# The fixed order of a state-space layer, rewritten: whole input products between scan and outputs, no row sums in the loop

## The chip, the cores and the metric

The kernel runs on one core of a Trainium2 chip. The metric is device time of one launch in microseconds (us). The core's engines are TensorE (PE, with its weight loads PEld), VectorE (DVE), ScalarE (ACT), GpSimd (POOL) and SyncE (SP), which issues nearly all DMAs of this kernel.

## The reference, cut

A trunk of two layers on x of 512 positions by 1024 columns, float32. Layer 0 mixes with a state-space layer (S5), layer 1 with forgetting attention; each is followed by a gated feed-forward layer with a short convolution. Scales, shifts and gates of every sublayer are a product of the conditioning vector c (adaLN).

```python
def adaln_params(c, w, b):
    mod = jax.nn.silu(c) @ w + b
    shift, scale, gate = jnp.split(mod, 3, axis=-1)

def s5_mixer(h, w_in, lam_re, lam_im, log_dt, b_re, b_im, c_re, c_im, d_skip, w_glu, w_out):
    u = h @ w_in
    ug = u.reshape(Bsz, S, S5_GROUPS, S5_GROUP)      # 64 groups of 16 channels
    ...                                              # lb = exp(lam dt), bb = k(lam, dt) * b, complex
    bu_re = jnp.einsum('blgc,gpc->blgp', u_c, bb_re) # a state of 64 complex numbers per group
    ...                                              # h[t] = lb * h[t-1] + bu[t]
    y = jnp.einsum('blgp,gcp->blgc', hs_re, cr) - jnp.einsum('blgp,gcp->blgc', hs_im, ci)
    y = y + d_skip * u
    y = jax.nn.gelu(y)
    y = y * jax.nn.sigmoid(y @ w_glu)
    return y @ w_out

for i in range(2):
    shift, scale, gate = adaln_params(c, ada_w[i, 0], ada_b[i, 0])
    h = h + gate * mixer_i(modulate(h, norm_g[i, 0], shift, scale))
    shift, scale, gate = adaln_params(c, ada_w[i, 1], ada_b[i, 1])
    h = h + gate * conv_ffn(modulate(h, norm_g[i, 1], shift, scale))
return rmsnorm(h, final_g)
```

## The kernel before

**Products.** Every float32 operand is split into a high part (`w_hi`, `a_xhi`: a rounding copy, mostly on ACT) and a rest (`w_lo`, `x_lo`: source minus high part, on DVE or POOL). A product is three matmuls per tile of 128 x 512: high by high, high by rest, rest by high. With 8 tiles of the inner dimension a 128-column output tile is 24 matmuls; in the state-space layer they are written by `mms` (L323).

**The state-space layer** is `s5`. It is written under a manual schedule: each engine runs its instructions in the order in which the program writes them, SP's DMAs too. SP is one queue: a DMA that waits for something holds up all that is written behind it.

The 1024 columns are 8 tiles m of 8 groups. The scan runs over blocks of 8 positions: 64 blocks a sequence. For each tile there are

- `inputs(m)`: 24 matmuls (L323) make tile m of u; ACT copies it to `uf`, `store_u` sends it to DRAM (`s_ud`), and `turn_u` reads it back turned (`u`). This load waits for the store.
- `s5_made` (L976 on DVE, L980 on POOL): the complex outer products `x` of decay powers and bb; `s5_states_out` (the same lines) those of c, `w2`. `s5_tables` (L966 to L968, POOL) makes the rotation tables in pieces.
- `s5_columns` (L1008, L1011, L1022 on PE): within-block responses and the transposed weights `w1`. ACT copies the first to `ktt`, PE turns it (L1026) to `kt`, SP stores it to DRAM (`s_z`).
- `s5_shifted`: SP loads the shifted response `tw` (L1037) from `s_z`, ACT masks it in 8 pieces to `t` (L1041).
- `s5_scan`: 32 small matmuls (L1053), then nine DVE instructions (L1070 to L1081), among them the scan (L1075), leave the block states `ua`.
- `s5_outputs`: u times t (L1091), w2 times `ua` (L1100), gelu on ACT (`yg`), a store to DRAM (`s_yd`). The gate product reads it back as `yt` (`s5_read_y`) and splits it to `a_hi`/`a_lo`.

The loop over m has one round for each tile. A round also parts one later tile of w_in (`parted`: high part on ACT, L1136, rest on POOL, L1138), and computes adaLN parameters of layer 1: one third as PE steps (`ada_pe`, four matmuls of 32 x 512 for each of the steps, L228), one third as row sums on DVE (`row` loads 512 KB, `row_sum` multiplies and adds, L265). In rounds 6 and 7, and behind the loop, the gate product of the first five output tiles is begun (`glu_head`, L1312), with its weights parted by `gate_hi` (ACT) and `gate_lo` (POOL, L1303). The stage after `s5` ("s5b") finishes the gate product and multiplies by w_out; then come the feed-forward layer, attention and the second feed-forward layer.

Of the kernel before, what the change touches and what calls it, by code (L numbers as in the profile page):

```python
# [63 lines left out]
class Trunk:  # L64
# [6 lines left out]
    def __init__(self, tc, io, ctx):  # L71
# [12 lines left out]
        self.acc = None  # L84
# [103 lines left out]
    def raw(self, shape, src, n=0):  # L188
        if n == 2:
            t = self.rest(shape, F32, "raw")  # L190
        else:
            t = self.wpool.tile(shape, F32, name="raw", tag=("raw", "w_hi")[n], bufs=(RAW, WB)[n])
        self.nc.sync.dma_start(t, src)
        return t
# [92 lines left out]
    def split(self, src, shape, pool=None, bufs=WB, off=None):  # L287
# [9 lines left out]
        self.put_parts(hi, lo, self.raw(shape, src), src if self.by_dma else None)  # L297
# [519 lines left out]
class S5(Trunk):  # L817
# [36 lines left out]
    def s5_params(self, pool, tp, prm, stats):  # L854
# [7 lines left out]
        ring = lambda n: tp.tile([P, (24, 36, 24)[n], H], F32, name=f"s5_ring{n}")  # L862
# [247 lines left out]
    def s5_read_y(self, pool, m, bufs=2):  # L1110
        nc = self.nc
        t = pool.tile([P, L, B], F32, name="yt", bufs=bufs)
        nc.sync.dma_start(t, self.yd[m].rearrange("g c i b -> (g c) i b"))
        return t.rearrange("p i b -> p (i b)")

    def s5(self, i, nxt):
# [5 lines left out]
        with ExitStack() as stack:  # L1122
# [11 lines left out]
            def parted(m):  # L1134
                hi = self.wpool.tile([P, KT, P], F32R, name="w_hi", bufs=WB)
                nc.scalar.activation(hi, w[m], AF.Copy)  # L1136
                lo = self.rest([P, KT, P])
                nc.gpsimd.tensor_tensor(lo, w[m], hi.bitcast(F32), ALU.subtract)  # L1138
                w[m] = [(hi[:, k], lo[:, k]) for k in range(KT)]

            with ExitStack() as start:
# [36 lines left out]
                self.s5_tables(slice(0, 8), 3, 5)  # L1178

                shift = self.ada_pe(i, (0,), late=True)  # L1180
                ps = self.mm.tile([P, S], F32, name="mmp")
                for k in range(KT):
                    if k % 2 == 0:
                        next(shift)
# [9 lines left out]
                load_w(1)  # L1194
# [17 lines left out]
                def part_x(k):  # L1212
                    b = self.par[i][:, k:k + 1]
                    nc.scalar.activation(xhi[:, k], x[:, k], AF.Identity, bias=b)
                    nc.vector.scalar_tensor_tensor(
                        xlo[k], x[:, k], b, xhi[:, k].bitcast(F32), op0=ALU.add, op1=ALU.subtract
                    )

                w2s[0] = self.s5_states_out(0)
                for k in range(3):  # L1220
                    part_x(k)
# [7 lines left out]
                parted(1)  # L1229
                self.s5_tables(slice(0, 8), 5, 6)  # L1230
                ws[0] = next(cols[0])
                for k in range(3, KT):
                    part_x(k)
                self.spread_c()
                self.s5_signs(far)
            pool = self.s5r = spool("s5r", stack)

            def store_u(m, uf):
                nc.sync.dma_start(ud[m].rearrange("g c j b -> (g c) j b"), uf)

            def turn_u(m):
                us[m] = pool.tile([P, GM, B], F32, name="u", bufs=3)
                nc.sync.dma_start(us[m], ud[m].rearrange("g c j b -> (c j) g b"))

            def inputs(m):
                ps = self.mm.tile([P, S], F32, name="mmp")
                for k in range(KT):
                    self.mms(ps, w[m], split_x, k, KT, full)
                    if k == 4:
                        yield  # L1250
# [3 lines left out]
                yield  # L1254

            def shifted_in(m):
                ts[m] = self.s5_shifted(m)
                next(ts[m])

            def scan_in(m):  # L1260
                sts[m] = self.s5_scan(m, ws.pop(m), us[m])
                next(sts[m])

            def made(m):
                xs[m] = self.s5_made(m)

            def columns_in(m):
                cols[m] = self.s5_columns(m, xs.pop(m))
                if m + 1 < KT and m > 1:
                    self.s5_diagonal(m + 1)  # L1270
# [18 lines left out]
            def parts(m, e):  # L1289
                y = yt.pop(m)  # L1290
                nc.scalar.activation(yhi[:, m], y, AF.Copy)
                e.tensor_tensor(ylo[:, m], y, yhi[:, m].bitcast(F32), ALU.subtract)

            def gate_load(n):
                raw[n] = self.raw([P, KT, P], self.io["s5_w_glu"][n], 2 * (n == HEAD - 1))

            def gate_hi(n):
                hi[n] = self.wpool.tile([P, KT, P], F32R, name="w_hi", bufs=WB)
                nc.scalar.activation(hi[n], raw[n], AF.Copy)

            def gate_lo(n):
                lo[n] = self.rest([P, KT, P])
                nc.gpsimd.tensor_tensor(lo[n], raw[n], hi[n].bitcast(F32), ALU.subtract)  # L1303
# [12 lines left out]
            store_u(0, uf)  # L1316
            load_w(2)
            turn_u(0)
            next(cols[0])
            made(1)  # L1320
            shifted_in(0)
            u1 = inputs(1)
            next(u1)
            next(u1)
            load_w(3)
            self.load_c()
            columns_in(1)
            next(ada)
            row()
            turn_u(1)  # L1330
            parted(2)
            scan_in(0)
            ts[0] = next(ts[0])
            for m in range(KT):
                more = m + 1 < KT
                if more:
                    ws[m + 1] = next(cols[m + 1])
                if m + 3 < KT:
                    parted(m + 3)
                if m + 2 < KT:  # L1340
                    up = inputs(m + 2)
                    next(up)
# [4 lines left out]
                if more:  # L1347
# [432 lines left out]
```

## Time and profile before

| | us |
|---|---|
| median of three runs | 1202.3 |
| the three runs | 1200.47, 1202.3, 1207.83 |
| the profiled execution's own time | 1208.57 |
| its span in the trace | 1206.8 |
| PE busy in the span | 1168.7 (97%) |
| DVE, ACT, POOL busy | 956.8, 649.1, 223.9 |
| mean granted clock of PE | 0.982 of full |
| DRAM traffic | 202.72 MB, 168 GB/s |

Durations in the prediction come from the one profiled execution, which is 6.3 us above the median of the runs. In rows of the trace, "L12" is line 12 of the kernel before; names read output <- inputs.

### The profile page before, as it was taken

To read this page: it belongs to the slowest core of one execution; us is meant where nothing else is said; L and a number is where in the kernel's file an instruction comes from. 1 tells how busy PE (TensorE), PEld (TensorE's weight loads), DVE (VectorE), ACT (ScalarE), POOL (GpSimd) and SP (SyncE) were. 2 spreads that over 40 slices of the span, in tenths; PEclk is the share of its full clock that TensorE was granted. 3 is DMA by queue.
4 is the path that set the end of the run, shared out by engine and by line. 5 is a ranking of instruction groups with operands and counts; after the bars stand their busy time and mean duration, and the time that the engine had idled before them with its cause. 6 is when DMAs were issued, how large, how long until landed. Compare 5 with 4: busy or idle time off the path is not lost.

```text
span 1206.8 us, 21348 instructions
## 1 busy us (share of the span) xinstructions
PE 1168.7 (97%) x8223; PEld 1038.5 (86%) x8223; DVE 956.8 (79%) x1733; ACT 649.1 (54%) x1165; POOL 223.9 (19%) x273
## 2 busy tenths in 40 slices
PE   7899987999999999999999999999999999999997
PEld 2577866899999999999899788878999899999987
DVE  8876755979998798887676788876899888898855
ACT  3562452535576666666543566654456555555543
POOL 5677653000011111111000343330000000000000
PEclk9997888999999999999999999999999999999999
DMA  9576576953598898998604654623122332333331
GB/s 353 193 244 206 179 231 217 312 187 102 139 249 239 218 259 230 261 241 230 190 23 132 219 180 162 201 89 93 50 88 93 110 125 86 110 123 92 105 88 71
DMA packets 79717, 202.72 MB, mean 168 GB/s; under 512 B 23951, under 2 KB 26479, under 8 KB 78591
## 3 DMA queue, kind: packets, MB, share of 16 engines
q1 hardware_dynamic: 73135, 181.96, 45.5%
q0 software_dynamic: 6192, 18.88, 9.1%
q8 instruction: 64, 1.05, 0.4%
q10 hardware_dynamic: 288, 0.52, 0.1%
q14 instruction: 38, 0.31, 0.1%
HBM read 194.41 MB, written 6.92 MB: 167 GB/s over the span
## 4 chain that ended last, share of the span: by engine, by line
PE 78%; DVE 11%; DMA 4%; issue 2%; ACT 2%; POOL 2%; SPq 0%; DVEq 0%; POOLq 0%; ACTq 0%
PE mmp L323 39%; PE mmp L583 16%; PE aux L583 6%; PE mmp L1521 3%; DMA raw<-in_w_up 2%; DVE w_lo L307 2%; PE aux L1667 2%; PE aux L1650 1%; PE mmp L1312 1%; DVE sums L554 1%; PE aux L1100 1%; DVE conv L637 1%; PE aux L1620 1%; PE mmp L1156 1%; PE aux L1091 1%
## 5 line engine op out<-in xcount | busy, mean ns | idle before, releaser
L302 ACT ACTIVATE w_hi<-raw 128x1024 fp32r<-128x1024 f32 (+4 forms) x196 | 172.2, 887 | 134.7 <-PE mmp L323 63.9
L307 DVE TENSOR_TENSOR w_lo<-raw,w_hi 128x1024 fp32r<-128x1024 f32 (+4 forms) x153 | 155.1, 1016 | 37.5 <-ACT w_hi L302 33.7
L323 PE MATMUL mmp<-ghi,w_hi 128*128 128x512 f32 (+1 forms) x392 | 144.1, 368 | 0.0
L323 PE MATMUL mmp<-glo,w_hi 128*128 128x512 f32 (+1 forms) x392 | 143.7, 367 | 0.0
L323 PE MATMUL mmp<-ghi,w_lo 128*128 128x512 f32 (+1 forms) x392 | 143.6, 366 | 0.0
L323 PE MATMUL mmp<-a_hi,w_hi 128*128 128x256 f32 (+1 forms) x440 | 141.1, 323 | 0.7 <-ACT nm_t L1435 0.7
L323 PE MATMUL mmp<-a_hi,w_lo 128*128 128x256 f32 (+1 forms) x440 | 139.0, 317 | 0.0
L323 PE MATMUL mmp<-a_lo,w_hi 128*128 128x256 f32 (+1 forms) x440 | 138.8, 316 | 0.0
L583 PE MATMUL mmp<-w_hi 128*128 128x256 f32 x420 | 116.9, 278 | 3.1 <-ACT nm_h L590 3.0
L583 PE MATMUL mmp<-w_hi,w_lo 128*128 128x256 f32 x420 | 116.1, 276 | 0.0
L583 PE MATMUL mmp<-w_lo,w_hi 128*128 128x256 f32 x420 | 116.0, 276 | 0.0
L265 DVE CUSTOM_DVE_ANT_0 ada_raw<-ada_raw,ada_c,rest 128x1024 f32<-128x1024 f32 x72 | 102.1, 1431 | 9.8 <-DMA ada_raw<-in_ada_rows 9.8
L302 ACT ACTIVATE w_hi<-sums 128x1024 fp32r<-128x1024 f32 x78 | 81.8, 1058 | 45.2 <-DVE sums L554 27.8
L307 DVE TENSOR_TENSOR w_lo<-sums,w_hi 128x1024 fp32r<-128x1024 f32 x78 | 94.4, 1219 | 4.5 <-ACT w_hi L302 3.1
L323 PEld LDWEIGHTS mmp<-a_hi,w_hi 128*128 128x128 f32 x440 | 82.2, 188 | 8.2 <-issue 2.6
L323 PEld LDWEIGHTS mmp<-a_hi,w_lo 128*128 128x128 f32 x440 | 82.6, 188 | 6.4
L323 PEld LDWEIGHTS mmp<-a_lo,w_hi 128*128 128x128 f32 x440 | 82.7, 188 | 4.6
L323 PEld LDWEIGHTS mmp<-ghi,w_lo 128*128 128x128 f32 x392 | 73.6, 188 | 12.3
L323 PEld LDWEIGHTS mmp<-ghi,w_hi 128*128 128x128 f32 x392 | 73.6, 188 | 11.2
L323 PEld LDWEIGHTS mmp<-glo,w_hi 128*128 128x128 f32 x392 | 73.6, 188 | 11.1
L583 PEld LDWEIGHTS mmp<-w_hi 128*128 128x128 f32 x420 | 78.8, 188 | 4.5 <-ACT nm_h L590 4.3
L583 PEld LDWEIGHTS mmp<-w_hi,w_lo 128*128 128x128 f32 x420 | 78.8, 188 | 0.1
(332 smaller groups left out, 3196.2 us busy)
## 6 DMA issues: line engine op xcount, KB each, us to landing
raw<-in_w_up SPq DMA_DIRECT2D x88, 512.0 KB, 3.6
ada_raw<-in_ada_rows SPq DMA_DIRECT2D x72, 512.0 KB, 4.8
raw<-in_ada_w SPq DMA_DIRECT2D x24, 512.0 KB, 7.9
raw<-in_w_down SPq DMA_DIRECT2D x32, 384.0 KB, 3.8
raw<-in_w_down SPq DMA_DIRECT2D x32, 320.0 KB, 3.3
nf<-nfd SPq DMA_DIRECT2D x8, 1152.0 KB, 5.7
w_lo<-in_w_up POOLq DMA_DIRECT2D x17, 512.0 KB, 8.2
raw<-in_fox_qk SPq DMA_DIRECT2D x16, 512.0 KB, 3.3
```

The costliest lines, as they stand in the source:

```text
L265: nc.vector.tensor_tensor_reduce(w, w, self.crow, 1.0, self.ada_b[:, i, m:m + 1], ALU.mult, ALU.add, self.par[i][:, m:m + 1])
L302: nc.scalar.activation(hi, src, AF.Copy)
L307: self.late = (nc.vector.tensor_tensor(lo, src, hi.bitcast(F32), ALU.subtract).ins,)
L323: self.last_mm = self.nc.tensor.matmul(o, wt, xt[:, cols], start=(k == 0 and n == 0), stop=(k == nk - 1 and n == 2),)
L554: sub = lambda o, u, v, op=ALU.subtract: nc.vector.tensor_tensor(o, u, v, op)
L583: self.last_mm = nc.tensor.matmul(o, wt[:, k], xt[:, k], start=(first and k == 0 and n == 0), stop=(k == H - 1 and n == 2), skip_group_che ...
L637: nc.vector.scalar_tensor_tensor(t[:, d:], ps[:, :S - d], cw[:, 2 - d, f:f + 1], t[:, d:], op0=ALU.mult, op1=ALU.add)
L1091: nc.tensor.matmul(yp[g2][:, k, :], t[:, 2 * k + g2], u[:, g, :], start=(k == 0), stop=False, skip_group_check=True,)
L1100: nc.tensor.matmul(yp[g2][:, k, 1:], w2[rows, k, r].rearrange("p c i -> p (c i)"), st[rows, r, k, :B - 1], start=False, stop=(r == 1), til ...
L1156: nc.tensor.matmul(ps, self.ones, sq, start=(k == 0), stop=(k == KT - 1))
L1521: self.last_mm = nc.tensor.matmul(ps[q, b][:, :n], xt[:, k, tb], wt, start=(k == 0 and i == 0), stop=(k == KT - 1 and i == 2),)
L1667: nc.tensor.matmul(pv[:, c * P:], self.v[:, hp, k, r].rearrange("p t d -> p (t d)"), pp[:, r, c + 3 * k:NB + 3 * k, :].rearrange("p b t -> ...
```

## The change

It is all in `s5`, but for a few lines that hand things to it:

1. `inputs(m)` is written whole. Before, 15 of its 24 matmuls stood ahead of L1091, and 9 behind L1100.
2. Scale and shift of layer 1 (two thirds) are both computed by PE steps: eight `ada_step`, two in each of the rounds 0 to 2, one in rounds 3 and 4, each with two loads of 512 KB issued two steps ahead. The eight row sums of layer 1 (L265) and their loads are gone; five of layer 0 stay, behind the loop.
3. `rested`, the subtraction on POOL, is written a round behind `parted`, the copy on ACT.
4. The prologue loads and parts w_in tile 1 earlier, sends u of tile 0 earlier, writes inputs(1) ahead of the loop, and has DVE make two of eight `a_xhi`; table pieces of the first tiles move ahead.
5. Loads of gate weights and y for the gate product are written at the start of round 5 (before: rounds 4 and 5, behind other DMAs); their parts are spread over rounds 5 and 6; the rests of y are DVE's, not POOL's. Gate weights 5 to 7 are loaded ahead (`loaded`).

**PE, one round.** In the kernel before, behind the first 15 input matmuls of a round (L323, the names are operands of the split product; L228 is the layer-1 step):

```order
L1026 MATMUL aux<-rest,ktt 128x128
L1091 MATMUL aux<-u,t 128x64 x8
L228 MATMUL mmp<-raw,sc_85 32x512 x4
L1100 MATMUL aux<-ua,w_526 128x63 x16
L323 MATMUL mmp<-a_xhi,w_hi 128x512
L323 MATMUL mmp<-x_lo,w_hi 128x512
L323 MATMUL mmp<-a_xhi,w_lo 128x512
```

In the changed kernel, from the last input matmul of round 1 to the first of round 2 (L1161 is now the step):

```order
L323 MATMUL mmp<-a_xhi,w_lo 128x512
L1026 MATMUL aux<-rest,ktt 128x128
L1091 MATMUL aux<-u,t 128x64 x8
L1100 MATMUL aux<-ua,w_848 128x63 x16
L1161 MATMUL mmp<-raw,sc_85 32x512 x4
L1053 MATMUL aux<-u,w_916 64x64 x16
L1008 MATMUL aux<-dd,rest 128x128
L1011 MATMUL aux<-x,s_cd_133 32x128 x8
L1022 MATMUL aux<-rest,x 128x128 x8
L1161 MATMUL mmp<-raw,sc_85 32x512 x4
L323 MATMUL mmp<-a_xhi,w_hi 128x512
```

The nine matmuls that separated L1100 from the next L1053 now stand ahead of L1026.

**SP, one round.** The DMAs of round 1 before (`in_ada_rows` feeds a row sum, `in_ada_w` a step, `s_w_in` a later inputs):

```order
L193 DMA raw<-in_s_w_in 128x1024
L193 DMA raw<-in_ada_w 128x1024 x2
L258 DMA ada_raw<-in_ada_rows 128x1024
L1107 DMA s_yd<-yg 128x8x64
L1239 DMA s_ud<-uf 128x512
L1000 DMA dd<-in_s_dd 128x128
L1243 DMA u<-s_ud 128x8x64
L1028 DMA s_z<-kt 128x128
L1037 DMA tw<-s_z 128x1024
```

And after (L1260 is the store of u, L1264 its turned load):

```order
L1107 DMA s_yd<-yg 128x8x64
L193 DMA raw<-in_ada_w 128x1024 x2
L1000 DMA dd<-in_s_dd 128x128
L193 DMA raw<-in_ada_w 128x1024 x2
L193 DMA raw<-in_s_w_in 128x1024
L1260 DMA s_ud<-uf 128x512
L1264 DMA u<-s_ud 128x8x64
L1028 DMA s_z<-kt 128x128
L1037 DMA tw<-s_z 128x1024
```

The row sum's load is gone, a second pair of step loads has come, and all loads now stand ahead of the store of u.

**DVE, between two scans.** Before:

```order
L1081 TENSOR_TENSOR ua<-aux,ub 128x512
L976 TENSOR_TENSOR x<-mmp,s_bb 128x1024
L976 TENSOR_TENSOR x_814<-mmp,s_bb 128x1024
L976 TENSOR_TENSOR w_834<-mmp,s_cc 128x1024
L976 TENSOR_TENSOR x_835<-mmp,s_cc 128x1024
L265 ISA ada_raw,par_97<-ada_raw,ada_c,rest 128x1024
L265 ISA par_97 128x1
L1070 TENSOR_TENSOR m_936<-aux,s_rot 128x512
```

After:

```order
L1081 TENSOR_TENSOR ua<-aux,ub 128x512
L976 TENSOR_TENSOR x<-mmp,s_bb 128x1024
L976 TENSOR_TENSOR x_844<-mmp,s_bb 128x1024
L976 TENSOR_TENSOR w_848<-mmp,s_cc 128x1024
L976 TENSOR_TENSOR x_849<-mmp,s_cc 128x1024
L1070 TENSOR_TENSOR m_890<-aux,s_rot 128x512
```

The row sum that stood ahead of the scan's first instruction is gone. Behind `s5` the order of all engines is the same but for the preloaded gate weights.

The diff, cut to its core:

```diff
+            def rested(m):
+                src, hi = w[m]
                 lo = self.rest([P, KT, P])
-                nc.gpsimd.tensor_tensor(lo, w[m], hi.bitcast(F32), ALU.subtract)
+                nc.gpsimd.tensor_tensor(lo, src, hi.bitcast(F32), ALU.subtract)
...
+            def ada_step():
+                k = KT - len(steps)
+                steps.pop()
...
+                for t, wt in enumerate(ada.pop(k)):
+                    for q in range(2):
+                        qq = 2 * t + q
+                        nc.tensor.matmul(
+                            ada["ps"][32 * qq:32 * qq + 32, :], self.sc32[:, k, :], wt[:, q * S:(q + 1) * S],
...
+                if k + 2 < KT:
+                    ada_load(k + 2)
...
-                    if k == 4:
-                        yield
...
-            ada = self.ada_pe(i + 1, (0,), ahead=True)
-            units = [(i + 1, 8 + m) for m in range(8)] + [(i, 16 + m) for m in range(5)]
+            units = [(i, 16 + m) for m in range(5)]
...
             for m in range(KT):
-                more = m + 1 < KT
-                if more:
-                    ws[m + 1] = next(cols[m + 1])
-                if m + 3 < KT:
-                    parted(m + 3)
-                if m + 2 < KT:
-                    up = inputs(m + 2)
-                    next(up)
+                sts[m] = self.s5_scan(m, ws.pop(m), us[m])
+                next(sts[m])
+                ts[m] = next(ts[m])
...
+                if m + 3 < KT:
+                    if m == 0:
+                        parted(3)
+                    rested(m + 3)
...
+                if m == KT - 3:
+                    read(0, 1, 2, 3)
+                    for n in range(3):
+                        gate_load(n)
...
+                sts[m] = next(sts[m])
+                if m == 0:
+                    ada_step()
+                elif m + 1 < KT:
+                    columns_in(m + 1)
+                    if m < 3:
+                        ada_step()
+                if m + 4 < KT:
+                    load_w(m + 4)
+                if m == KT - 3:
+                    gate_hi(0, 1)
+                    gate_lo(nc.gpsimd, 0)
+                if m + 2 < KT:
+                    inputs(m + 2)
+                    turn_u(m + 2)
...
                 outs[m] = self.s5_outputs(m, us.pop(m), ts.pop(m))
                 next(outs[m])
...
-                sts[m] = next(sts[m])
-                if m + 4 < KT:
-                    load_w(m + 4)
-                next(ada, None)
-                next(ada, None)
-                row()
                 outs[m].send((w2s.pop(m), sts.pop(m)))
-                if m + 2 < KT:
-                    made(m + 2)
-                    next(up)
-                    columns_in(m + 2)
...
-                if more:
-                    w2s[m + 1] = self.s5_states_out(m + 1)
-                    row_sum()
-                    scan_in(m + 1)
-                    ts[m + 1] = next(ts[m + 1])
+                if m + 4 < KT:
+                    parted(m + 4)
+                if steps:
+                    ada_step()
+                if m + 2 < KT:
+                    xs[m + 2] = self.s5_made(m + 2)
...
+                if m + 1 < KT:
+                    w2s[m + 1] = self.s5_states_out(m + 1)
+                if m == KT - 3:
+                    y_lo(nc.vector, 0, 1, 2, 3)
+                    gate_lo(nc.gpsimd, 2)
```

More of the change, by code (lines that the diff above doesn't have):

```diff
@@ L296, in split @@
             lo = self.rest(shape, odd=self.odd)
[L297 removed]
+        self.put_parts(hi, lo, self.loaded.pop(0) if self.loaded else self.raw(shape, src), src if self.by_dma else None)
         return hi, lo
@@ L1183, in s5 @@
                     if k % 2 == 0:
+                        next(shift)
+                        if k == KT - 2:
+                            load_w(1)
+                            parted(1)
                         next(shift)
@@ L1287, in read, with y_hi, y_lo, gate_hi @@
                     yt[m] = self.s5_read_y(pool, m, 4)
[L1289 to L1292, printed above, removed]
-            def gate_load(n):
[L1295 to L1303, printed above, removed]
+            def y_hi(*ms):
+                for m in ms:
+                    nc.scalar.activation(yhi[:, m], yt[m], AF.Copy)
+            def y_lo(e, *ms):
+                for m in ms:
+                    e.tensor_tensor(ylo[:, m], yt.pop(m), yhi[:, m].bitcast(F32), ALU.subtract)
+            def gate_load(n):
+                raw[n] = self.raw([P, KT, P], self.io["s5_w_glu"][n])
+            def gate_hi(*ns):
+                for n in ns:
+                    hi[n] = self.wpool.tile([P, KT, P], F32R, name="w_hi", bufs=WB)
+                    nc.scalar.activation(hi[n], raw[n], AF.Copy)
+            def gate_lo(e, *ns):
+                for n in ns:
+                    lo[n] = self.rest([P, KT, P])
+                    e.tensor_tensor(lo[n], raw[n], hi[n].bitcast(F32), ALU.subtract)
             def glu_head(k, part, ms=range(HEAD)):
@@ new lines, in s5 @@
+                    for k in range(4, 6):
+                        glu_head(k, 0)
+                if m + 1 < KT:
+                    if m == 0:
+                        columns_in(1)
+                    next(cols[m + 1])
+                    ts[m + 1] = self.s5_shifted(m + 1)
+                    next(ts[m + 1])
+                if m == KT - 3:
+                    self.rooms, self.rests = WB, 3
+                    yhi = self.normed("a_hi", WHOLE)
+                    ylo = self.normed("a_lo", WHOLE)
+                    y_hi(0, 1, 2, 3)
+                    gate_hi(2)
@@ L1411, in s5 @@
                 glu_head(k, 1)
-            for _ in range(3):
-                row_sum()
-                row()
-            parts(KT - 1, nc.vector)
+            row_sum()
+            row()
+            y_hi(KT - 1)
+            y_lo(nc.vector, KT - 1)
             while rows:
@@ L1418, in s5 @@
                 row()
+            for n in range(HEAD + 1, KT):
+                gate_load(n)
+                self.loaded.append(raw[n])
             gps[HEAD] = self.aux.tile([P, S], F32, name="aux")
@@ L1440, in glu @@
                 )
-            for m in range(HEAD + 1):
-                glu(m, gps[m], slice(0, S))
-            self.product(self.io["s5_w_glu"], range(HEAD + 1, KT), KT, (yhi, ylo), glu, ticks=1)
-            self.load_x(resid)
+            with self.behind(headed):
+                for m in range(HEAD + 1):
+                    glu(m, gps[m], slice(0, S))
+                self.product(self.io["s5_w_glu"], range(HEAD + 1, KT), KT, (yhi, ylo), glu, ticks=1)
+            with self.behind(last_y):
+                self.load_x(resid)
             self.done()
```

188 lines of the change are left out of this document (99 added, 89 removed).

## The prediction

> **What bounds the kernel now.** I read the span first, then one row for each stretch of the program, then the chain that ended last inside the bad stretches, then the waits, then single instructions for prices.
>
> ```profile
> span 1206.8 us, 21348 instructions
> ```
> ```profile
> 38.00:52.20 14.20, 10.97 (x70) 7.69 (x69) 11.56 (x10) 13.13 (x24) 8.97 (x5) 1.00 0.26 79
> 52.20:69.20 17.00, 15.53 (x141) 12.30 (x141) 9.80 (x14) 8.63 (x21) 10.73 (x10) 0.90 0.78 257
> 69.20:83.10 13.90, 13.65 (x140) 10.88 (x139) 13.32 (x17) 7.21 (x20) 12.42 (x7) 1.00 0.69 218
> 83.10:102.30 19.20, 18.29 (x142) 13.79 (x141) 13.81 (x17) 7.18 (x20) 15.11 (x11) 0.75 0.69 222
> 102.30:120.20 17.90, 17.05 (x152) 13.42 (x151) 12.30 (x15) 7.97 (x22) 11.25 (x6) 0.89 0.72 226
> 120.20:136.10 15.90, 15.47 (x133) 12.65 (x133) 12.15 (x15) 7.18 (x20) 9.21 (x9) 0.82 0.54 162
> 136.10:149.90 13.80, 13.80 (x158) 11.92 (x159) 11.42 (x15) 6.86 (x21) 9.15 (x6) 0.96 0.63 194
> 149.90:167.70 17.80, 13.72 (x107) 10.43 (x103) 10.03 (x13) 10.70 (x24) 12.23 (x7) 0.81 0.79 260
> 167.70:206.40 38.70, 32.59 (x186) 25.70 (x184) 19.73 (x24) 10.38 (x24) 17.40 (x13) 0.91 0.64 217
> 206.40:1206.80 1000.40, 987.44 (x6892) 907.83 (x6892) 809.93 (x1452) 558.44 (x949) 95.45 (x131) 1.00 0.52 154
> ```
>
> Columns: from:to, length, busy time of PE, its weight loads, DVE, ACT and POOL (instructions in brackets), granted clock, DMA share, GB/s. Row 1 is the end of the prologue; rows 2 to 7 are rounds 0 to 5 of the state-space loop, cut where L1053 starts; row 8 is round 6, row 9 round 7 with the head of the gate product. The last row is everything else: PE busy 98.7% at full clock, and there the change moves no work, so I put it at zero. What can change lies in the 168 us above it, and shows two losses: PE idles, and its clock falls below 1.00.
>
> The chain of waits names what ends the idle time:
>
> ```profile
> 82.68 2.19 DVE ada_raw L265
> ...
> 150.28 4.71 DMA yt<-s_yd
> ...
> 180.68 8.98 POOL w_lo L1303 x3
> ```
> ```profile
> PE mmp L1312 <- POOL w_lo L1303: 5.8, 3, 2.8
> PE aux L1091 <- DVE ua L1081: 4.1, 4, 2.3
> ```
>
> In the loop a row sum (L265) holds up DVE's scan, and PE stands at L1091/L1100 for its result; in the tail PE stands for the y parts and the gate weights' rests. The four L1091 waits cost 4.1 us as idle time and more as clock:
>
> ```profile
> 90.75 1.97 PE L1091 MATMUL aux<-u,t 128*128 128x64 f32 x16 [0.92 <-DVE ua L1081]
> ```
> ```profile
> 55.00:59.00 4.00, 3.76 (x28) 3.17 (x29) 3.76 (x7) 0.77 (x3) 2.50 (x2) 0.57 1.01 357
> 62.00:69.00 7.00, 7.00 (x66) 5.36 (x64) 2.44 (x3) 2.93 (x5) 5.86 (x8) 1.00 0.63 189
> 92.70:102.90 10.20, 10.20 (x62) 7.09 (x63) 5.45 (x5) 1.14 (x3) 8.81 (x9) 0.50 0.46 146
> 116.60:120.00 3.40, 3.40 (x9) 2.34 (x8) 1.27 (x2) 0.55 (x2) 3.40 (x2) 0.50 0.76 245
> 130.20:137.10 6.90, 6.90 (x47) 5.46 (x47) 5.48 (x5) 1.51 (x5) 6.74 (x6) 0.51 0.55 170
> 157.50:164.40 6.90, 6.49 (x18) 4.59 (x18) 3.14 (x3) 3.10 (x5) 6.90 (x5) 0.51 0.64 189
> 188.30:195.10 6.80, 5.39 (x13) 4.28 (x14) 5.94 (x6) 0.00 (x0) 4.77 (x6) 0.50 0.84 308
> ```
>
> Six spells at half clock: 3.4 (the first, which fills most of its row) + 10.2 + 3.4 + 6.9 + 6.9 + 6.8 = 37.6 us, half of which, some 18 beside the idle time in them, is lost: 3.0 a spell. Lengths are near multiples of 3.4. The spell at 92.7 follows the wait shown by 2 us; four such waits stand in the row of waits, and four spells in rounds 2 to 6. The row 62 to 69 holds the same small matmuls without an idle gap, and its clock stays 1.00.
>
> **The change, part by part.** Prices for one round come from round 1, full clock and nearly no idle:
>
> ```profile
> 69.19 1.15 PE L1053 MATMUL aux<-u,w 128*64 128x64 f32 x32
> ...
> 72.43 0.47 PE L323 MATMUL mmp<-a_xhi,w_hi 128*128 128x512 f32 x1
> ...
> 76.08 1.89 PE L1091 MATMUL aux<-u,t 128*128 128x64 f32 x16
> 77.90 1.06 PE L228 MATMUL mmp<-raw,sc 128*32 128x512 f32 x8
> 78.90 2.00 PE L1100 MATMUL aux<-ua,w 64*128 64x63 f32 x32
> 80.83 0.50 PE L323 MATMUL mmp<-a_xhi,w_hi 128*128 128x512 f32 x1
> ...
> 83.11 1.15 PE L1053 MATMUL aux<-u,w 128*64 128x64 f32 x32
> ```
>
> By start times: scan products and column work 3.24 (0.25 of it idle), fifteen input matmuls and the transpose 3.65, L1091 1.82, one layer-1 scale step 1.00, L1100 1.93, the other nine 2.28: 13.92, so 12.67 without step and idle.
>
> *Whole product behind the scan products.* Nothing is added or removed on PE. The 2.28 us of matmuls that stood behind L1100 now stand ahead of L1091.
>
> ```profile
> 82.60 2.27 DVE L265 CUSTOM_DVE_ANT_0 ada_raw<-ada_raw,ada_c,rest 128x1024 f32<-128x1024 f32 x1
> 84.81 0.68 DVE L1070 TENSOR_TENSOR m<-aux,s_rot 128x512 f32<-128x512 f32 x1
> 89.92 0.69 DVE L1081 TENSOR_TENSOR ua<-aux,ub 128x512 f32<-128x512 f32 x1
> ```
>
> The scan takes 84.81 to 90.61, 5.8 us. Its input is ready some 1.1 us after L1053 starts; L1091 came 6.9 us after it, and now comes 3.0 + 3.65 + 2.28 = 8.9 after, or 9.9 with a step between. So a scan that starts on time is 2 to 3 us early. *No row sums in the loop* takes the 2.27 away that made it late: DVE's round falls from the 13.3 us of round 1 to 11.0, below PE's 12.7. Those sums become four more scale steps on PE (eight, not four) at 1.00 each.
>
> Rounds 0 to 5 thus need 6 x 12.67 + 8 x 1.00 = 84.0 us of PE, where the rows give 97.7: **-13.7**, if nothing waits and the clock stays.
>
> *What is late next.* Moving the product puts the end of inputs(m+2) some 3 us nearer to the next round's products, but on SP's queue the store of u, the turned load of u (which waits for that store), the store of z and the load of tw stand in this order, and t and ktt behind tw on ACT. L1026 of the next round needs ktt.
>
> ```profile
> tw<-s_z SPq DMA_DIRECT2D x8, 512.0 KB, 4.7
> s_ud<-uf SPq DMA_DIRECT2D x8, 256.0 KB, 4.5
> s_z<-kt SPq DMA_DIRECT2D x8, 64.0 KB, 3.0
> ```
> ```profile
> DMA to landing us min/median/max: 3.1/4.7/6.0
> ```
> ```profile
> 104.09 2.59 ACT L1041 ACTIVATE t<-tw,rest 128x128 f32<-128x128 f32 x8
> ```
>
> Medians: 4.5 + 3.0 + 4.7 + 2.6, plus about 1.6 to issue and for ktt: 16.4. From the end of one whole product to the L1026 behind the next there is one round: 14.7 us twice (two steps), 13.7 three times, 12.7 once, 13.9 on average. With tw at its 3.1 and the two stores 1.5 quicker each, an estimate, the chain is 11.8. The medians were taken with up to four 512 KB loads issued right ahead of the u store; now the loads are issued 6 us ahead, so I take the middle, 14.1: nothing in rounds with two steps, 0.4 with one, 1.4 without, **+2.6** in all (bounds 0 and +15, six times the 2.5 of the medians).
>
> *Prologue.* PE idles 3.2 us of row 1, behind this:
>
> ```profile
> 43.30 3.05 ACT a_xhi L1214 x5
> ```
>
> Two of these five go to DVE, part 1 is split before, u of tile 0 is sent before, so inputs(1) runs unbroken and L1053 finds its u: **-3.2** (bounds -3.2 and 0; POOL's added table work, now ahead of x, could eat it).
>
> *Tail.* Rounds 6 and 7 take 56.5 us, 46.3 of them PE-busy; of that 6.5 + 5.4 = 11.9 at half clock, so the work is 40.4. Gate weights and y parts now start a round earlier, and y's rests leave POOL for DVE. I take half of the 10.2 idle as left, since ACT must still do gate parts, y parts, ktt and gelu in one order: 40.4 + 5.1 = 45.5, **-11** (bounds -16 and -6, where all the idle stays).
>
> *Rests a round ahead* takes POOL's waits for ACT away; PE waited only once for it, so I cost it at nothing, hidden behind the 12.7 us of PE. The preloaded gate weights 5 to 7 meet a PE that was busy there: nothing.
>
> *Half clock.* All the above is at full clock. With waits left in about three places (one before round 3, two in the tail) I take three spells of 3.0: **+9** (bounds 0 and +24, one for each round).
>
> The Trainium skill, "TensorE: Matmul & The Clock Gate", Part 1, lists half speed as coming after at least one idle window of about 3.4 us. The 3.4 us grain agrees with the rows here, the need for a whole idle window does not: 0.92 us idle were enough at 90 us. By that rule no spell would be left, and the sum would be 9 lower.
>
> **Sum** against the profiled execution's own 1208.6: -3.2 - 13.7 + 2.6 - 11 + 9 = -16.3, to 1192.3. That execution lies 6.3 above the median of the runs, 1202.3; less 16.3 this is **1186**.
>
> **Rivals.**
>
> *No spell left.* The scan is early everywhere, the clock stays: -25, 1177. The rule of the Trainium skill quoted above (TensorE: Matmul & The Clock Gate, Part 1) gives this case. For it: round 5, without a step, ran its work with no idle. Against: PE's thin stretch (L1091, L1100, a step, L1053, columns) is now 7 to 8 us in one piece, two windows without a wide product, so any gap there counts.
>
> *Half clock each round.* The thin stretch itself, or a short wait for it, drops the clock in eight rounds: +24 in place of +9 gives 1201; with one stretch of 3.4 each (eight times 1.7, +14) 1191. Middle 1196. For it: that long stretch; against: the row 62 to 69.
>
> *The transfers set each round* (the other side). L1026 waits for ktt six times, as worked out above at the medians: six stalls of 2.5, each followed by a spell of 3.0, is +33 in place of 2.6 + 9: 1207; with the tw load at its 6.0, six times 1.3 more: 1215. It decides from a chain of 15.5 us on, where six stalls of 1.6 and their spells equal the 28 gained. For it: 16.4 by medians; against: the queue is emptier when the store starts.
>
> *The loop does not gain.* POOL, at 9 to 15 us busy in a round, holds the tables and adds that DVE's next x and the scan need; row sums gone, the scan waits for POOL. Then only prologue and tail stay, -14, with two spells in the tail, +6: 1194; with the four added steps 1198.
>
> **How the numbers follow.** Forecast (1180 to 1191) 0.50; no spell 0.13; half clock each round 0.18; transfers 0.12; loop without gain 0.07. Range 1174 to 1202: it takes in all but the transfers and a part of the prologue's and the tail's outer bounds. A measurement here tells 1% (12 us) from nothing: faster is below 1190.3. The forecast but for its upper end and no spell give 0.61, the low end of half clock each round 0.05: 0.66. Slower (over 1214) is the upper end of the transfers, 0.06; the same 0.28.
>
> **What would show it.** L1053 of round 0 near 49 us, rounds of 12.7 to 15, end of the gate head near 180 to 188. No wait of L1091 for DVE's ua; if L1026 waits for ktt, or ACT's t for tw, in more than three rounds, the transfers' rival holds. Half clock in at most three spells, some 19 us, or in each round. Weights' rests (the old L1303) off the chain. The prediction is wrong if the stage after 206 grows by what was won (gate loads landing late), or if rounds run at 13 us and yet the clock is 0.8.

## The result and the profile after

The changed kernel takes 1209.4 us (median of 11 runs, 1203.8 to 1211.9), the kernel before 1202.3. The ratio is 1.0054, with a 95% interval from 1.0031 to 1.0077: slower by half a per cent, where 1186 had been forecast. Times here and below are medians; of the version both_split two of twelve executions took 2970 and 4251 us, for a reason that the record does not show, and are left out of its numbers.

The two profiles alone mislead. The profiled execution of the changed kernel is its fastest (1203.8), the one of the kernel before is among its slowest (1208.6). So each was profiled once more (1210.1 and 1203.1), and where the two profiles of a kernel differ both are given. The windows of the changed kernel, cut like those of before (prologue, rounds 0 to 7 at L1053, rest), with the same columns:

```profile
38.00:51.40 13.40, 13.40 (x70) 10.52 (x69) 12.42 (x11) 9.40 (x21) 8.05 (x4) 0.75 0.47 158
51.40:66.00 14.60, 14.60 (x148) 11.25 (x147) 11.68 (x15) 12.08 (x28) 10.14 (x9) 1.00 0.84 293
66.00:82.60 16.60, 14.94 (x151) 11.15 (x147) 10.06 (x13) 7.16 (x20) 14.96 (x13) 1.00 0.75 259
82.60:98.20 15.60, 14.93 (x151) 11.16 (x147) 10.07 (x13) 7.16 (x20) 9.46 (x7) 1.00 0.76 260
98.20:116.70 18.50, 16.05 (x143) 12.37 (x139) 10.07 (x13) 8.15 (x22) 12.00 (x11) 0.87 0.59 185
116.70:131.00 14.30, 14.30 (x145) 11.79 (x141) 10.06 (x13) 6.17 (x19) 6.34 (x3) 0.93 0.34 92
131.00:145.10 14.10, 13.63 (x146) 11.97 (x142) 8.24 (x13) 8.23 (x21) 5.94 (x5) 1.00 0.75 259
145.10:169.70 24.60, 16.53 (x123) 14.11 (x123) 19.92 (x18) 11.06 (x27) 15.92 (x7) 0.66 0.55 187
169.70:202.50 32.80, 30.84 (x186) 25.57 (x184) 16.09 (x24) 9.94 (x23) 2.84 (x7) 0.94 0.53 182
202.50:1201.90 999.40, 987.41 (x6892) 907.46 (x6892) 808.55 (x1452) 558.15 (x948) 96.54 (x131) 1.00 0.52 155
```

DVE is down to 10 us in rounds 1 to 4 from some 12 to 14, as forecast, and the last row is what it was. But round 6 takes 24.6 us in place of 18.5 (from its first L1053 at 149.14; the prediction's row of 17.8 starts 0.8 later, and its row of round 5 is as much too long), and PE idles in rounds 1 to 3 (14.94 busy of 16.60 in round 1). The second profile has this round 6:

```profile
149.90:172.80 22.90, 15.03 (x125) 12.47 (x124) 18.05 (x19) 9.24 (x24) 13.62 (x6) 0.81 0.56 190
```

What PE and ACT wait for (us in total, times, longest), from the waits of the first profile between 38 and 210 us:

```profile
PE aux L1026 <- ACT ktt L1016: 4.8, 3, 2.4
PE aux L1091 <- DVE ua L1081: 4.7, 1, 4.7
```
```profile
ACT t L1041 <- DMA tw<-s_z: 25.5, 6, 5.9
```

Of the four waits of L1091 for the scan, those of rounds 2 to 4 are gone; that of round 6 has grown from 2.3 to 4.7. L1026 now waits for ktt in rounds 1, 2 and 3, and behind this wait stands ACT, which waits for tw six times. The order of SP shows why, in round 1:

```profile
79.00 0.33 SPq L1260 DMA_DIRECT2D s_ud<-uf  x1
83.59 0.38 SPq L1264 DMA_DIRECT2D u<-s_ud  x1
84.06 0.53 SPq L1028 DMA_DIRECT2D s_z<-kt  x1
86.86 0.32 SPq L1037 DMA_DIRECT2D tw<-s_z  x1
```
```profile
77.59 0.33 PE L1026 MATMUL aux<-rest,ktt 128*128 128x128 f32 x1 [1.66 <-ACT ktt L1016]
```
```profile
78.39 0.58 ACT L1313 ACTIVATE uf<-mmp 128x512 f32<-128x512 f32 x1
...
90.46 2.58 ACT L1041 ACTIVATE t<-tw,rest 128x128 f32<-128x128 f32 x8 [5.22 <-DMA tw<-s_z]
92.84 0.31 ACT L1016 ACTIVATE ktt<-aux 128x128 f32<-128x128 f32 x1
93.05 1.05 ACT L1023 ACTIVATE w<-aux 128x512 f32<-128x512 f32 x2
93.99 0.58 ACT L1313 ACTIVATE uf<-mmp 128x512 f32<-128x512 f32 x1
```

From 79.00 SP stands 4.6 us for the landing of the u store; only then go the store of z (2.8) and the load of tw (3.6), then ACT makes t and ktt, and behind those, in ACT's order, the next uf, with whose store all begins again. It is a ring, and from uf to uf it takes 15.6 us, where PE's work for this round is 14.7. PE's product for uf had ended at 75.9, where L1026 began to wait; uf came 2.5 us later, for it stood behind t, ktt and w.

Round 6 is told by DVE, and by POOL beside it:

```profile
147.01 9.69 DVE L1344 TENSOR_TENSOR a_lo<-yt,a_hi 128x512 fp32r<-128x512 f32 x4
156.62 0.68 DVE L1070 TENSOR_TENSOR m<-aux,s_rot 128x512 f32<-128x512 f32 x1
...
184.89 0.69 DVE L1344 TENSOR_TENSOR a_lo<-yt,a_hi 128x512 fp32r<-128x512 f32 x1 [5.27 <-ACT a_hi L1340]
```
```profile
147.77 2.81 POOL L1357 TENSOR_TENSOR w_lo<-raw,w_hi 128x1024 fp32r<-128x1024 f32 x1
150.55 2.81 POOL L980 TENSOR_TENSOR w<-w,x 128x1024 f32<-128x1024 f32 x1
153.32 2.83 POOL L1357 TENSOR_TENSOR w_lo<-raw,w_hi 128x1024 fp32r<-128x1024 f32 x1
```

Four rests of y, which the change gave to DVE, stand ahead of the scan of tile 6, whose products were begun at 145.1 us. Each takes 2.42 us while POOL subtracts and adds, and a later one takes 0.69 us at 184.89, when POOL has long been done (its last row ends at 172.9). So the scan starts at 156.62, and L1091 of round 6 waits for it.

The granted clock, over many executions, says the same from another side. With full and half speed alone, as in the windows of these traces, a clock of c over a span means that 2(1 - c) of the span ran at half speed: 33.9 us on average before (25 executions, median clock 0.986; 33.5 and 32.5 in the two other series), 48.5 in the changed kernel (11 executions, 0.980). Half of the 14.6 us more is 7.3, about the 7 us by which the medians differ. By this estimate the two kernels would be equal at full clock: what the change takes from DVE it gives back in waits, and the clock then charges for the waits.

### The profile page after: what moved, and what is told of

It is laid out like the page before. It is cut to its first block, busy times and chain, and to the rows that moved or that the text cites. A ratio compares the mean times of both kernels' runs of the same rounds, so it can differ in the third digit from the quotient of the medians.

```text
span 1201.9 us, 21406 instructions
## 1 busy us (share of the span) xinstructions
PE 1165.8 (97%) x8255; PEld 1038.7 (86%) x8255; DVE 950.2 (79%) x1726; ACT 649.6 (54%) x1169; POOL 206.7 (17%) x266
## 4 chain that ended last, share of the span: by engine, by line
PE 76%; DVE 10%; DMA 6%; ACT 3%; issue 2%; POOL 1%; SPq 0%; DVEq 0%; ACTq 0%; POOLq 0%
PE mmp L323 40%; PE mmp L583 15%; PE aux L583 6%; PE mmp L1582 3%; DMA raw<-in_w_up 2%; DVE w_lo L307 2%; PE aux L1728 2%; PE aux L1711 1%; PE aux L1100 1%; PE aux L1091 1%; DVE ada_raw L265 1%; DVE sums L554 1%; PE aux L1681 1%; DMA yt<-s_yd 1%; DMA raw<-in_s_w_in 1%
## 5 line engine op out<-in xcount | busy, mean ns | idle before, releaser
L323 PE MATMUL mmp<-ghi,w_hi 128*128 128x512 f32 (+1 forms) x392 | 144.1, 368 | 0.0
L323 PE MATMUL mmp<-glo,w_hi 128*128 128x512 f32 (+1 forms) x392 | 143.7, 367 | 0.0
L323 PE MATMUL mmp<-ghi,w_lo 128*128 128x512 f32 (+1 forms) x392 | 143.6, 366 | 0.0
L323 PE MATMUL mmp<-a_hi,w_hi 128*128 128x256 f32 (+1 forms) x440 | 141.1, 323 | 1.1 <-ACT nm_t L1494 1.1
L323 PE MATMUL mmp<-a_hi,w_lo 128*128 128x256 f32 (+1 forms) x440 | 139.0, 317 | 0.0
L323 PE MATMUL mmp<-a_lo,w_hi 128*128 128x256 f32 (+1 forms) x440 | 138.8, 316 | 0.0
L323 PEld LDWEIGHTS mmp<-a_hi,w_hi 128*128 128x128 f32 x440 | 82.2, 188 | 8.6 <-issue 2.5
L265 DVE CUSTOM_DVE_ANT_0 ada_raw<-ada_raw,ada_c,rest 128x1024 f32<-128x1024 f32 x64 | 84.0, 1327 | 5.9 <-DMA ada_raw<-in_ada_rows 5.9
L323 PEld LDWEIGHTS mmp<-a_hi,w_lo 128*128 128x128 f32 x440 | 82.6, 188 | 6.4
L323 PEld LDWEIGHTS mmp<-a_lo,w_hi 128*128 128x128 f32 x440 | 82.8, 188 | 4.6
L323 PEld LDWEIGHTS mmp<-ghi,w_lo 128*128 128x128 f32 x392 | 73.6, 188 | 12.3
L323 PEld LDWEIGHTS mmp<-ghi,w_hi 128*128 128x128 f32 x392 | 73.6, 188 | 11.2
L323 PEld LDWEIGHTS mmp<-glo,w_hi 128*128 128x128 f32 x392 | 73.6, 188 | 11.1
L554 DVE TENSOR_TENSOR sums<-raw 128x512 f32<-128x512 f32 x70 | 46.0, 686 | 41.5 <-DMA raw<-in_w_up 41.4
```

The costliest lines, as they stand in the source:

```text
L265: nc.vector.tensor_tensor_reduce(w, w, self.crow, 1.0, self.ada_b[:, i, m:m + 1], ALU.mult, ALU.add, self.par[i][:, m:m + 1])
L323: self.last_mm = self.nc.tensor.matmul(o, wt, xt[:, cols], start=(k == 0 and n == 0), stop=(k == nk - 1 and n == 2),)
L554: sub = lambda o, u, v, op=ALU.subtract: nc.vector.tensor_tensor(o, u, v, op)
```

## The experiments

The theories: **transfers** (SP's order makes tw and ktt late), **tail** (DVE's y rests hold up round 6), and **clock** (the long stretch of small matmuls lowers the clock by itself). Ratios are to the kernel before on the same chip.

**tw_first: z and tw ahead of the turned u.**

```diff
                     inputs(m + 2)
-                    turn_u(m + 2)
...
                     ts[m + 1] = self.s5_shifted(m + 1)
                     next(ts[m + 1])
+                if m + 2 < KT:
+                    turn_u(m + 2)
```

> Changed kernel, with the store of z and the load of tw issued ahead of the turned load of u. Transfers theory (the loop's left-over waits come from SP's order, the u store's landing stands ahead of z and tw): ACT's waits for tw fall from 25.5 us to under 10, L1026 no longer waits for ktt (4.8 us in the changed kernel's profile), and the spells behind those waits go: 5 to 10 us under the changed kernel's median of 1209.4. Clock theory (the long stretch of small matmuls drops the clock by itself): the waits go too, but half clock stays near 50 us and the time falls by 3 us at most. Tail theory (what is lost is lost in rounds 6 and 7): the loop gets faster by its 5 us, the tail stays 58 us long.

Measured: 1200.1 us, ratio 0.9992 (0.9976 to 1.0008), 9 us under the changed kernel. Waits of ACT and of PE in its profile:

```profile
ACT t L1041 <- DMA tw<-s_z: 7.8, 5, 2.4
```
```profile
PE aux L1026 <- ACT ktt L1016: 1.3, 1, 1.3
```

25.5 has become 7.8, and 4.8 has become 1.3. The gain is more than twice the 3.5 us of waits: half clock falls too, from 48.5 to 41.0 us on average. The order of the DMAs in one queue was worth more than the whole change lost. The 3 us that the clock theory allowed are exceeded. The 4.6 us are not all gained: the store of z is now issued 0.4 us behind the u store and lands after 5.7 us (median), not 2.6, and the load of tw waits for it. From the issue of the u store to that of the tw load it was 7.9 us in round 1 and is 6.8 here; the ring from uf to uf takes 15.2 and 15.0 in rounds 1 to 3, where it took 15.6 and 16.2.

**ylo_late: the rests of y behind the scan of tile 6.**

```diff
                 sts[m] = next(sts[m])
+                if m == KT - 2:
+                    y_lo(nc.vector, 0, 1, 2, 3)
...
                 if m == KT - 3:
-                    y_lo(nc.vector, 0, 1, 2, 3)
                     gate_lo(nc.gpsimd, 2)
```

> Changed kernel, with DVE's four rests of y (L1344, 9.69 us in one row) behind the scan of tile 6 and not ahead of it. Tail theory: the scan of tile 6 starts some 9 us sooner after its L1053, the 4.7 us wait of L1091 for ua goes, a shorter wait of the gate matmuls for a_lo takes its place: 3 to 8 us under 1209.4. Clock theory: the tail's half clock stays, gain under 2 us.

Measured: 1203.0 us, ratio 1.0011 (0.9996 to 1.0026), 6 us under the changed kernel. DVE in round 6:

```profile
149.83 0.68 DVE L1070 TENSOR_TENSOR m<-aux,s_rot 128x512 f32<-128x512 f32 x1
...
156.12 3.84 DVE L1344 TENSOR_TENSOR a_lo<-yt,a_hi 128x512 fp32r<-128x512 f32 x4
```

The scan starts 2 us behind its products at 147.9, not 11.5, and the same four rests, with POOL busy only until 157.6, take 0.96 us each. The tail theory holds.

**no_rests: POOL quieter beside the rests of y.** The subtraction for gate weights 1 and 2 is left out, all else as changed.

```diff
                 for n in ns:
+                    if n in (1, 2):
+                        self.rests += 1
+                        lo[n] = hi[n]
+                        continue
```

> Changed kernel without the subtraction that makes the rests of gate weights 1 and 2 on POOL (the high parts stand in for them; the matmuls stay). Tail theory with a shared path between DVE and POOL: the four rests of y on DVE take 0.7 to 1.2 us each and not 2.42, since POOL is quiet beside them but for one add; the scan of tile 6 starts 5 to 7 us sooner, the time falls 4 to 8 us. If the slowness of L1344 has another cause (its operands), it stays at 9 to 10 us and the time within 1.

Measured: 1205.9 us, ratio 1.0032 (1.0009 to 1.0056), 3.5 us under the changed kernel.

```profile
152.16 5.78 DVE L1344 TENSOR_TENSOR a_lo<-yt,a_hi 128x512 fp32r<-128x512 f32 x4
```

1.45 us each, with two adds of POOL left beside them, 4.0 of the 5.8 us. So the same DVE instruction, on tiles of the same shape, takes 0.69 us with POOL idle, 1.45 with POOL partly busy, 2.42 with POOL busy throughout; in the changed kernel's second profile it takes 1.85, with POOL busy for 6.2 of 7.4 us. The scan starts 7.2 us behind its products (11.5 and 9.8 in the changed kernel's profiles). The expected 0.7 to 1.2 was too low, and the time just missed its range; the direction is the theory's.

**split: the input product in two parts again.**

```diff
                 for k in range(KT):
                     self.mms(ps, w[m], split_x, k, KT, full)
+                    if k == 4:
+                        yield
...
                 outs[m].send((w2s.pop(m), sts.pop(m)))
...
+                if m + 2 < KT:
+                    next(up)
+                    turn_u(m + 2)
```

> Changed kernel with the input product split again, 15 matmuls ahead of the outputs and 9 behind, and the turned load of u behind those; all else as changed. Clock theory: the thin stretch is cut in two, half clock falls by 10 us or more (clock 0.983 or higher), and the time falls 3 to 8 us. Theory that the whole product is what gains: L1091 waits for the scan again where DVE is late, and t comes later with the later u: 3 to 10 us slower than 1209.4.

Measured: 1210.0 us, ratio 1.0078 (1.0053 to 1.0104), no different from the changed kernel. Half clock falls by 8 us (40.7 on average), yet the time does not. PE waits for something new:

```profile
PE mmp L323 <- ACT uf L1315: 4.9, 2, 3.2
```

Neither expectation came true as written. In rounds 0 to 5 L1091 does not wait for the scan, although the product is split; what stands against the clock's gain in this profile is that PE waits until ACT has copied an earlier product to uf.

**both: tw_first and ylo_late together.** The edits are those two.

> Changed kernel with both edits that were faster alone: the store of z and the load of tw ahead of the turned load of u (1200.1 alone), and DVE's four rests of y behind the scan of tile 6 (1203.0 alone), against 1209.4. If the two losses are separate (one in the loop, one in the tail), the gains add: 1193 to 1195, under the kernel before. If both only shift where the clock drops, the sum is no better than the better one: 1199 to 1201.

Measured: 1193.1 us, ratio 0.9924 (0.9895 to 0.9953), 16 us under the changed kernel and 9 under the kernel before. By the medians 9.2 + 6.3 = 15.5; by the ratios 0.62% and 0.43% make 1.05% of the 1.30% that both bring, within the intervals. The two losses are separate and add up. Its windows (prologue, rounds 0 to 5, round 6, round 7 with the head; the last runs 3.5 us into the next stage, whose first product starts at 192.48, against 207.01 and 205.01 in the two profiles of before):

```profile
38.00:51.40 13.40, 13.40 (x71) 10.74 (x70) 11.93 (x12) 9.39 (x21) 8.88 (x5) 0.75 0.44 151
51.40:141.60 90.20, 88.06 (x861) 69.69 (x860) 58.21 (x76) 50.02 (x131) 59.68 (x45) 0.96 0.73 235
141.60:160.70 19.10, 13.40 (x127) 11.14 (x126) 13.51 (x19) 9.98 (x25) 12.76 (x6) 0.82 0.66 208
160.70:196.00 35.30, 32.71 (x201) 27.09 (x200) 20.84 (x29) 13.16 (x28) 3.34 (x7) 1.00 0.64 221
```

Half clock is down to 25.8 us on average (6 executions), below the kernel before.

**before_no_sums: the kernel before without the row sums of layer 1** and their eight loads (that part of the scale is left out).

```diff
-            units = [(i + 1, 8 + m) for m in range(8)] + [(i, 16 + m) for m in range(5)]
+            units = [(i, 16 + m) for m in range(5)]
...
                     w2s[m + 1] = self.s5_states_out(m + 1)
-                    row_sum()
```

> Kernel before, without the eight row sums of layer 1 and their loads (their part of the scale is left out), nothing in their place. Theory of the prediction (the sums on DVE hold up the scan): L1091 waits less for ua, and the time falls 6 to 12 us under the kernel before (1201). Rival (u and t arrive through the queue at the same time, so PE waits for those instead): under 3 us.

Measured: 1193.5 us, ratio 0.9936 (0.9915 to 0.9957): 9 us by the medians, 5 to 10 by the interval. Taking the sums away is worth what was thought, but this run takes their 4 MB of loads out of the queue too, and does not tell the two apart. That the sums held up the scan is shown in part: the waits of L1091 for ua fall from 4.1 us to 2.2, not to nothing, and 0.4 us stays in each of rounds 3 and 4 (one profile, of its slowest execution, 1202.6).

**before_again and after_again: both kernels unchanged.**

> Kernel before, unchanged, for a profile of a usual execution, since the first one was among its slowest (1208.6 against a median of 1201). Clock theory: its loop then holds three to five spells of half clock, 28 to 36 us in the whole span, against some 49 in a usual execution of the changed kernel; L1053 of round 0 at 51 to 52 us and of round 6 at 144 to 147. Ratio 1.000.

> Changed kernel, unchanged, for a profile of a usual execution, since the first one was its fastest (1203.8 against 1209.4). Clock theory: 45 to 53 us at half clock, the four to six spells in rounds 2 to 7 behind waits for ktt, yg and ua. Transfers theory: ktt is waited for in at least three rounds again, 4 us or more. Ratio about 1.006.

Measured: 1203.6 (ratio 1.0000, 0.9981 to 1.0020) and 1209.8 (1.0060, 1.0038 to 1.0081). The second pair of profiles:

```profile
52.50:149.20 96.70, 92.74 (x828) 74.21 (x828) 72.27 (x90) 44.56 (x122) 66.85 (x46) 0.88 0.67 213
149.20:167.70 18.50, 14.47 (x123) 11.01 (x123) 10.58 (x15) 11.41 (x25) 12.49 (x7) 0.82 0.83 272
```

These are rounds 0 to 5 and round 6 of the kernel before. In the changed kernel's second profile round 0 starts at 51.8 and round 6 at 150.0, so its loop takes 98.2 us where this one takes 96.7; its round 6, shown above, takes 22.9 where this one takes 18.5. In the first pair the loop had been 93.6 against 96.9 (from the first L1053 to that of round 6). In the changed kernel the place of the clock's spells moves from one execution to the next, and the loop's time with it; in the kernel before both profiles have six spells from 38 us on, 37.5 us in all, at almost the same places.

**both_split: the version with both edits, with the product split** (the edit of split).

> The version with both edits (1193.1), with the input product split again, 15 matmuls ahead of the outputs and 9 behind. Theory that the whole product gives the scan its time: L1091 waits for ua again and the u store comes 3 us later: 5 to 12 us slower, 1198 to 1205. Clock theory (the long stretch of small matmuls costs by itself): half clock, 25.8 us with both, falls to 20 or less, and the time to 1190 or under.

Measured: 1204.1 us, ratio 1.0015 (0.9991 to 1.0039), 11 us slower than with the product whole.

```profile
PE mmp L323 <- ACT uf L1315: 5.2, 2, 3.3
```

With the transfers in order the whole product is worth 11 us; in the changed kernel as it came it was worth nothing. But the reason is not the expected one: L1091 waits for ua nowhere in this profile, and PE again stands for uf. Half clock is 33.4 us on average, not less than with the whole product (25.8), so the clock theory fails here: cutting the long stretch of small matmuls in two did not bring the clock back.

**best: both edits, and the gate matmuls of y's rests behind the outputs.**

```diff
                 if m == KT - 2:
-                    for k in range(4):
-                        glu_head(k, 0, (0, 1))
+                    glu_half(yhi, True, (0, 1))
...
                 outs[m].send((w2s.pop(m), sts.pop(m)))
+                if m == KT - 3:
+                    y_hi(0, 1, 2, 3)
+                    gate_hi(2)
+                if m == KT - 2:
+                    glu_half(ylo, False, (0, 1))
```

> The version with both edits (1193.1), and in rounds 5 and 6: gelu of tile 5 ahead of the high parts of y on ACT, and the eight gate matmuls that need y's rests behind the outputs of tile 6, so that they no longer wait for DVE in front of them (4.9 us in that version's profile). Tail theory: that wait and the 1.0 us for yg go, 2 to 6 us faster, 1187 to 1191. If the scan of tile 6 then is what is waited for instead, L1100 waits 3 us or more for ua and the time stays within 2 us.

Measured: 1192.1 us, ratio 0.9914 (0.9882 to 0.9946). Against 1193.1 that is no difference that this measurement tells. The version with both edits had these waits, 4.7 us of them in round 6, and the new one does not:

```profile
PE mmp L1366 <- DVE a_lo L1344: 4.9, 2, 4.7
```

Round 6 still takes 19.0 us. In place of the wait L1026 stands 1.9 us for ktt and L1091 0.9 for ua, and 10.2 us are at half clock where the version with both edits has 6.8. That this is where the 4.7 us went is read from one profile of each.

**both_no_steps: both edits, without seven of the eight steps** and their loads.

```diff
-                    for q in range(2):
+                    for q in range(2 if k == 0 else 0):
...
-                    ada_load(k + 2)
+                    ada[k + 2] = ()
```

> The version with both edits (1193.1), without seven of the eight steps that compute scale and shift of layer 1 on PE, and without their loads (their part of the result is left out). If a step costs PE what its row says (1.0 us each): 7 us less, 1185 to 1187. If the steps also give the transfers their time (a shorter round makes ktt late): 2 to 5 us less. If their 7 MB of loads hold up the queue: 9 us or more.

Measured: 1180.7 us, ratio 0.9818 (0.9782 to 0.9853), 12.4 us less than both (7 to 18 by the intervals, from four executions): 1.8 us a step, not 1.0. It is over the 9 us that were expected if the loads count. Rounds 0 to 5 of its profile, to set beside the 90.20 us of both:

```profile
52.70:130.20 77.50, 77.22 (x805) 66.66 (x804) 58.97 (x79) 48.72 (x128) 58.66 (x44) 0.99 0.58 176
```

Of the 12.7 us between the two rows 1.9 are idle time (the waits for ktt are gone altogether) and, by the granted clocks, an estimated 2.8 are half speed; the 8.0 that are left make 1.1 us a step. So a step's own time is about its row; the rest of its price came as waits and as clock. Whether the loads or PE's longer rounds bring the waits, this run does not tell.

**both_part1: both edits, and the high part of tile 1 later on ACT.**

```diff
                         if k == KT - 2:
                             load_w(1)
-                            parted(1)
...
                 for k in range(3):
                     x_hi(k)
+                parted(1)
+                rested(1)
```

> The version with both edits (1193.1), with the high part of w_in tile 1 on ACT behind the first three of a_xhi, as in the kernel before, and not ahead of the copy of the adaLN rows. Clock theory for the prologue (the 0.6 us that PE stands at L170 in front of the many matmuls of one column starts the spell that every profile of the changed kernel has at 41.5 or 44.9 us): the spell goes in the profile, L1053 of round 0 starts at 49 to 50 us instead of 51.5, and the time falls 2 to 3 us. If the spell comes from those matmuls themselves: no change, within 1 us.

Measured: 1192.1 us, ratio 0.9914 (0.9886 to 0.9942), again 1 us. The spell in the prologue is gone from the profile, but L1053 of round 0 starts at 51.7 us as ever, because of this:

```profile
PE mmp L323 <- DVE x_lo L1254: 2.3, 2, 1.8
```

In this profile, at full clock, PE waits for the rests of x; in that of both, at half clock, it is slow enough not to wait. So the start of round 0 is set by DVE, not by the clock and not by what was moved.

## Why the prediction was wrong, point by point

- **The row sums** (-2.27 us a round on DVE, which held up the scan): right in size. before_no_sums gives 9 us, with the loads of the sums gone too, and in the changed kernel the waits of L1091 in rounds 0 to 5 are gone.
- **The whole product** (rounds 0 to 5 at 84.0 us of PE): worth 11 us, but only in an order in which the transfers keep up (both against both_split); in the kernel as changed it gave nothing (split). The mechanism was to give the scan 2 to 3 us more ahead of L1091, and that is not what the runs show: with the row sums gone and the product split again, L1091 waits for the scan in none of rounds 0 to 5. There PE stands for uf instead, 4.9 and 5.2 us.
- **"What is late next", +2.6**: this is the first step that failed. The chain was named, and its length was right (14.1 taken; 14.2 from the u store at 79.00 to the end of ktt at 93.2). But it was started at the end of PE's product. It starts at uf, and uf stands on ACT behind t, ktt and w, which end the same chain: uf came 2.5 us behind the product in round 1. So the chain closes to a ring of 15.6 us, and rounds with two steps, where I wrote "nothing", waited too (rounds 1 and 2). The other fault was the price: 2.6 us for the waits and the spells as a lump of three; taking most of 4.8 us of waits away brought 9.2. The rival "the transfers set each round", with 0.12, had the queue and the wait right, and by the prediction's own sign it holds (ACT's t waits for tw six times). Its size is not borne out: three stalls, 4.8 us in all, and not six of 2.5. That its 1207 to 1215 takes in the measured 1209.4 is partly luck, since some 6 us of that are the tail's, which it did not have.
- **The tail, -11**: the second step that failed. "y's rests leave POOL for DVE" was written down as relief. What was not counted is where they stand on DVE (ahead of a scan that PE waits for) and what they cost beside a busy POOL. The rows that would have warned were in the trace of before: a row sum on DVE took 2.27 us beside POOL's adds, in the row that the prediction quotes, and 1.27 us at 193.43, with POOL done (its row stands in the last section). The tail gained nothing, round 6 lost 4 to 6 us, and the edit that moves the rests brought 6.3.
- **The prologue, -3.2**: it gave 0.7 to 1.0 (L1053 at 51.5 and 51.8 in place of 52.2 and 52.7). I had taken PE's idle time there as removable; by the profile of both_part1 DVE's rests of x set the start.
- **The added steps, 1.0 us each**: 1.8 each by both_no_steps, of which about 1.1 is PE's own time. So the row was read rightly; what the steps cost beyond it belongs to the waits and to the clock.
- **Half clock, +9**: the direction was wrong. Three spells were kept of six; the changed kernel has 14.6 us more at half speed than before, on average. The Trainium skill's rule of a whole idle window ("TensorE: Matmul & The Clock Gate", Part 1) would have left at most the spell at the 4.7 us wait of round 6; the traces stand further from it than the prediction did: waits of 0.4 to 4.7 us were often, not always, followed by spells of one to four windows of 3.4 us.
- **The base**: the working took its idle time and its clock from one of the slowest executions of before (0.982, 43 us at half speed; on average it is 33.9). By this estimate some 5 us of what was to be won was not there in an average run. No profile shows such a run: the second one has the same clock, and of the 5.4 us by which it is faster only 2.0 lie ahead of the stage behind `s5` (205.01 against 207.01).

With the two failed steps mended, the kernel is 9 us faster than before. Where the rest of the 16.3 predicted is can be read from one profile of each, that of both and the second one of before. The prologue gives 1.3 (predicted 3.2). The loop gives 6.5 (predicted 8.1: 13.7 less 2.6 and one spell of 3.0). Round 6 and the head give 4.8 (predicted 5.0: 11 less two spells). That is 12.5; the stages behind took 0.9 longer, and the two profiles differ by 2.3 more than the medians do.

## What to carry to other kernels

When a stall is removed from an in-order schedule, walk each queue again behind the moved instruction, and ask of every DMA that waits for a landing what stands behind it: here one turned load, needed a whole round later, held up a load needed at once, and swapping them was worth 9 us. Work taken off one engine must be priced where it lands, next to what runs beside it and in front of what it stands. And where the matrix engine's clock falls after short waits, a wait can cost more than its length: 3.5 us fewer waits went with 9.2 us in tw_first. It is no fixed rate, since 4.9 us of waits taken out in best brought nothing that could be measured.

## What the runs showed of the hardware that was not expected

A VectorE subtraction of two tiles of 128x512 took 0.69 us with GpSimd idle, 1.45 us with GpSimd partly busy and 2.42 us with GpSimd subtracting and adding all the time. VectorE's outer products (L976), 128x1024, took 1.22 us beside the same GpSimd work; why they are not slowed is not shown. The row sum of the kernel before took 2.27 us beside GpSimd's adds, and without them:

```profile
193.43 1.27 DVE L265 CUSTOM_DVE_ANT_0 ada_raw<-ada_raw,ada_c,rest 128x1024 f32<-128x1024 f32 x1
```

It is not always VectorE that is slowed: at 186.16 a row sum took 1.28 us, and the GpSimd subtraction that began inside it, at 186.32 (L1303), took 3.3 us; the shortest of its four took 2.4.

Granted half clock came in stretches of 3.4 us and its multiples, in other places in the two profiles of the changed kernel, and in almost the same places in the two of the kernel before. Eleven runs of the changed kernel span 8 us, and their clocks go from 0.978 (1210.8 to 1211.9 us) to 0.984 (1203.8 us).
